# A chunked scan whose solve is made for two head pairs at once: one product with the states, one with block-diagonal inverses

## The chip, the cores and the metric

The kernel runs on one core of a Trainium2 chip. The metric is device microseconds of one execution; the time before is the median of three runs. A profile of one execution gives every instruction with its start and duration. The engines are named as in the profile: PE (TensorE, its matmuls), PEld (TensorE's weight loads), DVE (VectorE), ACT (ScalarE), POOL (GpSimd) and SP, whose queue issues the DMAs.

## The reference

One layer of a hybrid decoder over 528 positions (16 learned ones ahead of 512), width 2048, all fp32. The change touches the recurrence of its 16 heads of size 64, `rwkv7_scan`:

```python
# S_t = S_{t-1} diag(w_t) + (S_{t-1} a_t) b_t^T + v_t k_t^T ; y_t = S_t r_t
def step(s, inp):
    r_t, w_t, k_t, v_t, a_t, b_t = inp
    sa = jnp.einsum('bhvk,bhk->bhv', s, a_t)
    s = s * w_t[:, :, None, :] + sa[..., None] * b_t[:, :, None, :] + v_t[..., None] * k_t[:, :, None, :]
    y_t = jnp.einsum('bhvk,bhk->bhv', s, r_t)
    return s, y_t
```

Around it stand the layer's projections (`n @ w_in` with 6592 columns, `w_out`), a short convolution group beside the heads, a norm per head, and a feed-forward block (`w_gate_up`, a causal convolution, `w_down`).

## The kernel before, in words

Activations lie with features on partitions and time along the free axis. Every large product is made from splits of both operands (hi and lo, type float32r): three matmuls of 128x128 weights and about 258 moving columns for each tile, all into PSUM tiles named `mps`. The small products of the recurrence are plain fp32; such a matmul is two instructions in the trace.

**Pairs and chunks.** The 16 heads are 8 pairs P; a pair's two heads h lie on partitions 0 to 63 and 64 to 127. Two pairs (p = 0, 1) go through one scan s, so there are four scans, one after the other. Time is cut into NC = 17 chunks of C = 32 positions.

**prep(P)** fills `XR`, the moving side of the scan: for each head on its own 64 partitions the scaled vectors a (first 32 columns of a chunk) and r (last 32), and on the other 64 partitions their products with k and b, made by 64x64 matmuls (tile `aux`, from `bk`) and masked. **inverse(s)** turns the 68 small triangular matrices of a scan into their inverses on DVE and writes them to DRAM (`d2`); **inverses(s, i)**, called by `load`, brings them to the SBUF tile `AT` in two parts of 9 and 8 chunks, on SP's queue. **moves** copies k, b and v with transposes into `BK` and `VT`.

**scan(s)**, for every chunk c, works on `cur`, one of three tiles `SUV` of 128 x (2 pairs, 2 heads, 64): the state of a head on its own 64 partitions, and on the other 64 the values v (32 rows, put there by POOL) and the solved u (32 rows).

1. x0: for each pair one fp32 matmul with `cur[:, p]` as weights (128x128) and the chunk's a columns of both heads as 64 moving columns. The result lies with values on partitions; two DVE transposes of 64x64 bring the wanted blocks to `X0`.
2. u: for each pair one fp32 matmul of `AT` (128x128) with `X0`, 64 moving columns; four ACT copies of 32x64 bring u into `cur`.
3. State: four 64x64 matmuls (`BK` with `cur`), then DVE adds the decayed state `s0`, made by POOL, and writes the next `SUV`.
4. y: for each pair one fp32 matmul with `cur[:, p]` as weights and the r columns of both heads as 64 moving columns; two ACT copies write `yt`.

All four results are PSUM tiles named `st`, of which two are in turn.

**Order of the work.** Everything up to the output projection is only recorded first (`Plan.keep`). `Plan.order` then simulates the engines with the costs of `Plan.time` (an fp32 matmul of n columns in the full array counts n / 600 + 0.02 us, a matmul in a smaller mode 0.055, a change of mode 0.1 or 0.25) and gives out all instructions in the order found: work of the scan, prep, inverse and norm comes first when it is ready, and projection matmuls (`rkv`, `conv`, rank FILL) fill TensorE in between. After the last scan the norms of its two pairs (`head_norm`) run under the last projections, and the output projection follows. Nearly every instruction is recorded through one helper line, L218, so tiles are told apart by name.

Of the kernel before, what the change touches and what calls it, by code (L numbers as in the profile page):

```python
# [10 lines left out]
F32 = mybir.dt.float32  # L11
# [14 lines left out]
C = 32  # L26
# [195 lines left out]
class Plan:  # L222
# [51 lines left out]
    def time(self, x):  # L274

        e, op, out = x["engine"].name, x["op"], x["out"]
        n = 1
        for s in out.shape[1:] if isinstance(out, View) else (512,):
            n *= s
        psum = any(a.tile.pool.space == "psum" for a in x["ins"])  # L280
        if e == "PE":
            if self.mode(x) != (128, 128):
                return 0.055
            return n / 600 + 0.02 if x["args"][1].tile.dtype is F32 else n / 2400 + 0.0115
        if e == "SP":
            return 0.42
        if e == "POOL":
            if op == "memset":
                return 0.1 + 0.0008 * n
            if op == "tensor_scalar":  # L290
                return 0.3 + 0.0011 * n
            return 0.25 + 0.0019 * n if n > 300 else 0.2 + 0.0016 * n
        if e == "ACT":
            t = 0.15 + 0.00087 * n if psum else 0.19 + 0.00084 * n
            return t + (0.09 if isinstance(x["kw"].get("scale"), View) or isinstance(x["kw"].get("bias"), View) else 0)
        if op == "tensor_reduce":
            n = 1
            for s in x["kw"]["in_"].shape[1:]:
                n *= s
        if op == "tensor_tensor_scan":  # L300
            return 0.2 + 0.002 * n
        if op in ("tensor_scalar", "tensor_copy", "memset") and not psum:
            return 0.15 + 0.00055 * n
        if op == "transpose":
            return 0.19 + 0.00102 * n
        return 0.155 + 0.00104 * n + (0.06 if isinstance(x["kw"].get("scalar"), View) else 0)
# [167 lines left out]
def hymba(tc, I, out, ysp=None):  # L474
# [99 lines left out]
    with ExitStack() as ctx1:  # L574
# [8 lines left out]
            SUV.append(t)  # L583

        ATw = p1.tile([128, (2 * NC + 1) * 2 * C], F32, name="AT")
        G.memset(ATw, 0.0)
        AT = ATw[:, :NC * 4 * C].rearrange("r (c p b t) -> r c p b t", c=NC, p=2, b=2)
        X0 = []  # L590
        for i in range(2):
            t = p1.tile([128, 2, 2, C], F32, name=f"X0{i}")
            G.memset(t, 0.0)
            X0.append(t)

        xs = []
        ss = []
# [77 lines left out]
                PE.matmul(ps[:, :b - a], w, x[:, a:b], start=(i == 0), stop=(i == len(terms) - 1))  # L675
            return ps[:, :b - a]

        xr_shape = [128, 2, 2, NC, 64]
        lox = []

        def lora_in(t):
            if t == T_WD:
                wad = p1.tile(xr_shape, F32R, name="XR", bufs=2).rearrange("p a b c d -> p (a b c d)")
                wd, ad = inproj(t, HL), inproj(T_AD, HL, [
                    (wad[:, 1024 * i:1024 * i + 512], wad[:, 1024 * i + 512:1024 * i + 1024]) for i in range(KT // 4)])
                for _ in range(KT):
                    next(wd)
                    yield
                    if _ >= LAG:
                        next(ad)  # L690
                        yield
                for _ in range(max(0, LAG - LATE)):
                    next(ad)
                    yield
                ps0 = yield from wd
                rstd = p1.tile([128, L], F32, name="rstd")
                m, q = p1.tile([128, LP], F32, name="t1"), p1.tile([128, LP], F32, name="t2")
                for a, b in HL:
                    rms([x[:, a:b] for x in ss], rstd[:, a:b], m[:, a:b], q[:, a:b], aux, "aux")
                norm1.append(rstd)  # L700
                both = p1.tile(xr_shape, F32R, name="XR", bufs=2).rearrange("p a b c d -> p (a b c d)")
                lox.extend([both[:, i * L:i * L + L] for i in (2 * n, 2 * n + 1)] for n in range(4))
                tb = p1.tile([128, 2 * C * C + C], F32, name="tb")
                o = tb[:, :L]
                shift(ps0, t, o)
                S.activation(out=o, in_=o, func=AF.Tanh)
                split(o, *lox[0])
                o = tb[:, L:2 * L]
                shift((yield from ad), T_AD, o)
                split(o, *lox[1])  # L710
            else:
                o = p1.tile([128, 2 * C * C + C], F32, name="tb")[:, :L]
                yield from shifted(t, o)
                S.activation(out=o, in_=o, func=AF.Sigmoid)
                split(o, *lox[2 + t - T_GD])
# [42 lines left out]
        def prep(P):  # L758
            s, p = P // 2, P % 2
            if p == 0:  # L760
                st["s", s] = (p1.tile([128, 2, 2, NC, 64], F32, name="XR", bufs=2),
                              p1.tile([128, 2, NC], F32, name="PC", bufs=2))
            XR, PC = st["s", s]
            k, r, v = st.pop(("k", P)), st.pop(("r", P)), st.pop(("v", P))
# [36 lines left out]
            G.tensor_tensor(out=al, in0=kk, in1=al, op=ALU.mult)  # L801
            for h in range(2):
                q = slice(64 * h, 64 * h + 64)
                V.scalar_tensor_tensor(out=XR[q, h, p, :, :C], in0=chunked(kk[q]), scalar=-1.0,
                                       in1=Pp[q, :, :C], op0=ALU.mult, op1=ALU.mult)
            for h in range(2):
                q = slice(64 * h, 64 * h + 64)
                G.tensor_tensor(out=XR[q, h, p, :, C:], in0=chunked(r[q]), in1=Pp[q, :, 1:], op=ALU.mult)
            V.tensor_tensor(out=bk[:, :, :C], in0=chunked(k), in1=chunked(Pi), op=ALU.mult)
            V.tensor_tensor(out=bk[:, :, C:], in0=chunked(al), in1=chunked(Pi), op=ALU.mult)  # L810
            br = p1.tile([128, LP], F32, name="t3")
# [5 lines left out]
            for c0 in range(0, NC, 8):  # L817
                n = min(8, NC - c0)
                ps = aux.tile([128, 8, 64], F32, name="aux")
                for c in range(c0, c0 + n):  # L820
                    for h in range(2):
                        q = slice(64 * h, 64 * h + 64)
                        o = slice(64 - 64 * h, 128 - 64 * h)
                        PE.matmul(ps[o, c - c0], bk[q, c], XR[q, h, p, c], start=True, stop=True)
                for h in range(2):
                    o = slice(96 - 64 * h, 128 - 64 * h)
                    V.transpose(pt[32 - 32 * h:64 - 32 * h, c0:c0 + n], ps[o, :n, :C])
                    o = slice(64 - 64 * h, 128 - 64 * h)
                    V.tensor_tensor(out=XR[o, h, p, c0:c0 + n], in0=ps[o, :n],
                                    in1=gmask[o].unsqueeze(1).to_broadcast([64, n, 64]), op=ALU.mult)  # L830
                yield 0.05 * n * 2, PD3
            if p == 0:
                st["d1", s] = dp.tile([4 * NC, C, C], F32, name="d1", bufs=2)
# [3 lines left out]

            for h in range(2):
                q = slice(64 * h, 64 * h + 64)
                G.tensor_tensor(out=XR[q, h, p, 1:], in0=XR[q, h, p, 1:],  # L840
                                in1=PC[q, p, :NC - 1].unsqueeze(2).to_broadcast([64, NC - 1, 64]), op=ALU.mult)

            b_ = br[:, :L]
            for a, b, ps in blocksum(x):
# [36 lines left out]
        def inverses(s, i):  # L881
# [1 line left out]
            c0, c1 = CH[i]  # L883
            d2 = st["d2", s]
            for h in range(2):
                for b in range(2):
                    o = 64 * h + 32 * b
                    SP.dma_start(AT[o:o + 32, c0:c1, :, b].rearrange("s c p t -> s (c p) t"),
                                 d2[2 * (h * NC + c0):2 * (h * NC + c1)].rearrange("q s t -> s q t"))

        def piece(s, i, n):

# [68 lines left out]
        def scan(s):  # L961
# [4 lines left out]
            for c in range(NC):  # L966
# [8 lines left out]
                    if c == 0:  # L975
                        G.memset(cur[64 * h:64 * h + 64, :, h], 0.0)

                xp = stp.tile([128, 2, 2, C], F32, name="st")
                for p in range(2):
                    PE.matmul(xp[:, p], cur[:, p], XR[:, :, p, c, :C], start=True, stop=True)  # L980
                x0 = X0[c % 2]
                for h in range(2):
                    q = slice(64 * h, 64 * h + 64)
                    V.transpose(x0[q, :, h], xp[q, :, h])
                yield 0.2, D1 * f
                up = stp.tile([128, 2, 2, C], F32, name="st")
                for p in range(2):
                    w = 2 * C * (2 * c + p)
                    PE.matmul(up[:, p], ATw[:, w:w + 128], x0[:, p], start=True, stop=True)
                for h in range(2):  # L990
                    o = 96 - 64 * h
                    for b in range(2):
                        S.copy(cur[o:o + 32, :, h, C * b:C * b + C], up[C * b:C * b + C, :, h])
                yield 0.2, D2 * f
                if c == 1:
                    inverses(s, 1)
# [6 lines left out]
                if c < NC - 1:  # L1003
# [11 lines left out]
                    for h in range(2):  # L1015
# [2 lines left out]
                            V.tensor_tensor(out=nxt[q, :, h], in0=sp[q], in1=s0[q], op=ALU.add)  # L1018
                        else:
                            V.tensor_copy(nxt[q, :, h], sp[q])  # L1020
                yp = stp.tile([128, 2, 2, C], F32, name="st")
                for p in range(2):
                    PE.matmul(yp[:, p], cur[:, p], XR[:, :, p, c, C:], start=True, stop=True)
                n = min(C, L - c * C)
                for h in range(2):
                    q = slice(64 * h, 64 * h + 64)
                    S.copy(yt[q, :, c * C:c * C + n], yp[q, :, h, :n])
                if c == CH[0][1] - 1:
                    st["half", s] = True
                yield 0.75, D3 * f  # L1030
# [7 lines left out]
        def head_norm(P, tags):  # L1038
# [4 lines left out]
            ahead = P >= NP - 2  # L1043
            if ahead:
                if P % 2:
                    t = p1.tile(xr_shape, F32, name="XR", bufs=2).rearrange("p a b c d -> p (a b c d)")
                else:
                    t = p1.tile([128, 2 * C * C + C], F32, name="tb")
                bv, g = t[:, :L], t[:, L:2 * L]
# [819 lines left out]
```

## Time and profile before

| | |
|---|---|
| median of 3 runs | 2435.49 us (2435.47 to 2435.78) |
| profiled execution, its own time | 2438.57 us |
| its span in the profile | 2436.8 us |
| mean granted TensorE clock | 0.994 |
| PE busy | 2389.3 us (98%), 18546 matmul instructions |
| DVE busy | 1731.2 us (71%) |
| ACT busy | 1157.3 us (47%) |
| POOL busy | 659.0 us (27%) |
| the scans | from about 215 to 772 us of the span |

Rows of the timeline read: start in us, time from the first to the last instruction of the merged row, engine, line, operation, output tile <- input tiles, for matmuls the part of the array used (rows*columns), the shape, and the count. Rows of one tile read: count, then shortest/median/longest duration in ns, then first and last start in us. A row of waits reads: who waited for whom, us in total, times, longest. Because matmuls overlap, their cost is read from the starts of successive rows.

### The profile page before, as it was taken

How to read it: one execution, taken by the hardware profiler on the slowest of the kernel's cores; microseconds unless marked ns; L12 is line 12 of the kernel's file. 1: busy time of each engine (PE TensorE's matmuls, PEld its weight loads, DVE VectorE, ACT ScalarE, POOL GpSimd, SP SyncE). 2: the span in 40 equal slices, each digit the busy share in tenths (PEclk: the TensorE clock that was granted, in tenths of full speed). 3: DMA queues.
4: the chain of work that ended last, by engine and by line, in shares of the span. 5: the costliest groups of instructions: out<-in, count | busy, mean ns of one | idle time of the engine just before them, and what ended most of it. 6: DMA issues, size and time to landing. Idle time of an engine off the chain costs nothing.

```text
span 2436.8 us, 46251 instructions
## 1 busy us (share of the span) xinstructions
PE 2389.3 (98%) x18546; PEld 2283.9 (94%) x18546; DVE 1731.2 (71%) x2410; ACT 1157.3 (47%) x2139; POOL 659.0 (27%) x755
## 2 busy tenths in 40 slices
PE   7999999999999999999999999999999999999996
PEld 7999999999999999898999999998989898989896
DVE  6677888888865623786676767686868585959586
ACT  6666655656553433464443434343425252525254
POOL 2222646455442011441111212121212020202025
PEclk9999999999999999999999999999999999999998
DMA  5444332342442633423232324242424232323352
GB/s 175 148 130 123 89 88 82 101 110 86 119 124 77 201 92 120 153 84 104 78 122 85 122 75 127 70 130 70 138 70 130 78 122 87 110 90 103 98 193 71
DMA packets 138806, 266.64 MB, mean 109 GB/s; under 512 B 38592, under 2 KB 51648, under 8 KB 138592
## 3 DMA queue, kind: packets, MB, share of 16 engines
q1 hardware_dynamic: 138592, 263.69, 35.0%
q8 instruction: 146, 2.39, 0.4%
q14 instruction: 68, 0.56, 0.1%
HBM read 240.69 MB, written 22.95 MB: 108 GB/s over the span
## 4 chain that ended last, share of the span: by engine, by line
PE 90%; DVE 5%; DMA 2%; issue 1%; ACT 1%; SPq 0%; POOL 0%; DVEq 0%; ACTq 0%; POOLq 0%
PE mps L218 58%; PE u L218 16%; PE d L218 10%; PE st L218 5%; PE aux L218 2%; DVE acc L218 1%; DVE O L218 1%; DVE raw L218 1%; DMA raw<-w_in_dram 0%; DVE q L218 0%; DMA R<-w_down_dram 0%; DVE tt L218 0%; DMA l<-t 0%; DMA d<-tb 0%; PE psn L218 0%
## 5 line engine op out<-in xcount | busy, mean ns | idle before, releaser
L218 ACT CAST H<-R 128x1024 fp32r<-128x1024 f32 x373 | 391.9, 1051 | 455.3 <-PE u L218 172.6
L218 DVE TENSOR_TENSOR O<-R,H 128x1024 fp32r<-128x1024 f32 x373 | 488.9, 1311 | 109.8 <-ACT H L218 109.5
L218 PE MATMUL mps<-ahi,whi 128*128 128x258 f32 (+2 forms) x2048 | 406.1, 287 | 12.2 <-ACT whi L218 12.2
L218 PE MATMUL mps<-ahi,wlo 128*128 128x258 f32 (+2 forms) x2048 | 406.5, 287 | 1.7 <-DVE wlo L218 1.6
L218 PE MATMUL mps<-alo,whi 128*128 128x258 f32 (+2 forms) x2048 | 406.7, 287 | 0.3 <-DVE alo L218 0.3
L218 DVE TENSOR_TENSOR wlo<-raw,whi 128x512 fp32r<-128x512 f32 x289 | 209.2, 728 | 181.8 <-ACT whi L218 162.7
L218 PEld LDWEIGHTS mps<-ahi,whi 128*128 128x128 f32 x2048 | 311.1, 190 | 12.7 <-ACT whi L218 12.4
L218 PEld LDWEIGHTS mps<-ahi,wlo 128*128 128x128 f32 x2048 | 312.4, 190 | 2.4 <-DVE wlo L218 2.1
L218 PEld LDWEIGHTS mps<-alo,whi 128*128 128x128 f32 x2048 | 312.0, 190 | 0.9 <-DVE alo L218 0.5
L218 ACT CAST whi<-raw 128x512 fp32r<-128x512 f32 x289 | 178.2, 621 | 241.0 <-PE mps L218 187.5
L218 PE MATMUL mps<-tt,H 128*128 128x258 f32 x1968 | 263.3, 284 | 1.8 <-ACT q L218 1.8
L218 POOL TENSOR_TENSOR raw<-raw,rb 128x516 f32<-128x516 f32 (+1 forms) x45 | 92.8, 2064 | 627.5 <-DVE raw L218 583.5
L218 PE MATMUL mps<-alo,H 128*128 128x258 f32 x1032 | 255.2, 284 | 6.0 <-DVE alo L218 6.0
L218 PE MATMUL mps<-ahi,H 128*128 128x258 f32 x1032 | 255.1, 284 | 1.0 <-ACT q L218 1.0
L218 PEld LDWEIGHTS mps<-tt,H 128*128 128x128 f32 x1968 | 249.1, 190 | 2.0 <-ACT q L218 2.0
L218 POOL TENSOR_TENSOR R<-R 128x1024 f32<-128x1024 f32 x40 | 133.1, 3327 | 422.4 <-DVE R L218 422.4
L218 DVE TENSOR_TENSOR R<-R 128x1024 f32<-128x1024 f32 x120 | 209.0, 1741 | 1.1
L218 PEld LDWEIGHTS mps<-alo,H 128*128 128x128 f32 x1032 | 194.8, 190 | 6.8 <-DVE alo L218 6.2
L218 PEld LDWEIGHTS mps<-ahi,H 128*128 128x128 f32 x1032 | 195.4, 190 | 1.8 <-ACT q L218 1.2
L218 POOL TENSOR_SCALAR SUV<-VT 32x64 f32<-32x64 f32 x272 | 135.1, 497 | 206.7 <-PE st L218 181.1
L218 PE MATMUL mps<-ahi,O 128*128 128x258 f32 x1032 | 153.4, 284 | 0.0
L218 PE MATMUL mps<-tt,O 128*128 128x258 f32 x984 | 141.8, 283 | 0.0
(318 smaller groups left out, 4536.6 us busy)
## 6 DMA issues: line engine op xcount, KB each, us to landing
R<-w_gu_dram SPq DMA_DIRECT2D x176, 512.0 KB, 3.6
raw<-w_in_dram SPq DMA_DIRECT2D x208, 256.0 KB, 2.7
R<-w_down_dram SPq DMA_DIRECT2D x88, 512.0 KB, 4.4
raw<-w_out_dram SPq DMA_DIRECT2D x64, 256.0 KB, 2.6
l<-lo SPq DMA_DIRECT2D x24, 264.0 KB, 2.5
hsp<-acc SPq DMA_DIRECT2D x8, 512.0 KB
tt<-hsp SPq DMA_DIRECT2D x4, 1024.0 KB, 10.8
lo<-l SPq DMA_DIRECT2D x12, 264.0 KB, 3.5
```

What stands on the lines that cost most here:

```text
L218: return getattr(self.real, op)(*real, **{k: x.get() if isinstance(x, View) else x for k, x in kw.items()})
```

## The change

In the scan, x0 takes `XR`'s a columns of both pairs and both heads as weights (128 rows, 2 x 2 x 32 columns) and the whole of `cur` as 256 moving columns: one matmul. Of its result only the four diagonal blocks of 32x64 are used; four ACT copies put them one below another into `x0` (128 x 64), and the two transposes are gone. `AT` becomes one 128x128 block-diagonal matrix a chunk (four blocks of 32x32, one for each pair and head), and u is one matmul of it with `x0`. y is made by four matmuls, one for each pair and head, with `cur[:, p, h]` (128x64) as weights and 32 moving columns; the heads' results lie on partitions 0 to 63 and 64 to 127 (128x64 tiles of the array), and one ACT copy takes both. `XR` is laid out by chunk first; `AT` is loaded by as many DMAs, each of half the size, because no block is stored twice. The planner's cost of an fp32 matmul in the full array changes.

```diff
-            return n / 600 + 0.02 if x["args"][1].tile.dtype is F32 else n / 2400 + 0.0115
+            return max(0.222, n / 600 + 0.004) if x["args"][1].tile.dtype is F32 else n / 2400 + 0.0115
...
-        ATw = p1.tile([128, (2 * NC + 1) * 2 * C], F32, name="AT")
-        G.memset(ATw, 0.0)
-        AT = ATw[:, :NC * 4 * C].rearrange("r (c p b t) -> r c p b t", c=NC, p=2, b=2)
...
+        AT = p1.tile([128, NC, 2, 2, C], F32, name="AT")
+        G.memset(AT, 0.0)
...
-        xr_shape = [128, 2, 2, NC, 64]
+        xr_shape = [128, NC, 2, 2, 2, C]
...
-                V.scalar_tensor_tensor(out=XR[q, h, p, :, :C], in0=chunked(kk[q]), scalar=-1.0,
+                V.scalar_tensor_tensor(out=XR[q, :, 0, p, h], in0=chunked(kk[q]), scalar=-1.0,
...
-                G.tensor_tensor(out=XR[q, h, p, :, C:], in0=chunked(r[q]), in1=Pp[q, :, 1:], op=ALU.mult)
+                G.tensor_tensor(out=XR[q, :, 1, p, h], in0=chunked(r[q]), in1=Pp[q, :, 1:], op=ALU.mult)
...
             for h in range(2):
-                for b in range(2):
-                    o = 64 * h + 32 * b
-                    SP.dma_start(AT[o:o + 32, c0:c1, :, b].rearrange("s c p t -> s (c p) t"),
-                                 d2[2 * (h * NC + c0):2 * (h * NC + c1)].rearrange("q s t -> s q t"))
+                for p in range(2):
+                    o = 64 * p + 32 * h
+                    SP.dma_start(AT[o:o + 32, c0:c1, p, h],
+                                 d2[2 * (h * NC + c0) + p:2 * (h * NC + c1):2].rearrange("c s t -> s c t"))
...
-                xp = stp.tile([128, 2, 2, C], F32, name="st")
+                xp = stp.tile([128, 2, 2, 64], F32, name="st")
+                PE.matmul(xp, XR[:, c, 0].rearrange("r p h t -> r (p h t)"), cur, start=True, stop=True)
+                x0 = p1.tile([128, 64], F32, name="x0", bufs=2)
                 for p in range(2):
-                    PE.matmul(xp[:, p], cur[:, p], XR[:, :, p, c, :C], start=True, stop=True)
-                x0 = X0[c % 2]
-                for h in range(2):
-                    q = slice(64 * h, 64 * h + 64)
-                    V.transpose(x0[q, :, h], xp[q, :, h])
+                    for h in range(2):
+                        q = slice(64 * p + 32 * h, 64 * p + 32 * h + 32)
+                        S.copy(x0[q], xp[q, p, h])
                 yield 0.2, D1 * f
-                up = stp.tile([128, 2, 2, C], F32, name="st")
+                up = stp.tile([128, 64], F32, name="st")
+                PE.matmul(up, AT[:, c].rearrange("r p h t -> r (p h t)"), x0, start=True, stop=True)
                 for p in range(2):
-                    w = 2 * C * (2 * c + p)
-                    PE.matmul(up[:, p], ATw[:, w:w + 128], x0[:, p], start=True, stop=True)
-                for h in range(2):
-                    o = 96 - 64 * h
-                    for b in range(2):
-                        S.copy(cur[o:o + 32, :, h, C * b:C * b + C], up[C * b:C * b + C, :, h])
+                    for h in range(2):
+                        S.copy(cur[96 - 64 * h:128 - 64 * h, p, h], up[64 * p + 32 * h:64 * p + 32 * h + 32])
...
-                yp = stp.tile([128, 2, 2, C], F32, name="st")
+                yp = stp.tile([128, 2, C], F32, name="st")
                 for p in range(2):
-                    PE.matmul(yp[:, p], cur[:, p], XR[:, :, p, c, C:], start=True, stop=True)
+                    for h in range(2):
+                        q = slice(64 * h, 64 * h + 64)
+                        PE.matmul(yp[q, p], cur[:, p, h], XR[:, c, 1, p, h], start=True, stop=True)
                 n = min(C, L - c * C)
-                for h in range(2):
-                    q = slice(64 * h, 64 * h + 64)
-                    S.copy(yt[q, :, c * C:c * C + n], yp[q, :, h, :n])
+                S.copy(yt[:, :, c * C:c * C + n], yp[:, :, :n])
```

The other lines of the diff rewrite reads and writes of `XR` for its new layout.

More of the change, by code (lines that the diff above doesn't have):

```diff
@@ L583, in hymba @@
             SUV.append(t)
-        ATw = p1.tile([128, (2 * NC + 1) * 2 * C], F32, name="AT")
-        G.memset(ATw, 0.0)
-        AT = ATw[:, :NC * 4 * C].rearrange("r (c p b t) -> r c p b t", c=NC, p=2, b=2)
[L590 to L594, printed above, removed]
+        AT = p1.tile([128, NC, 2, 2, C], F32, name="AT")
+        G.memset(AT, 0.0)
         xs = []
@@ L682, in lora_in @@
             if t == T_WD:
-                wad = p1.tile(xr_shape, F32R, name="XR", bufs=2).rearrange("p a b c d -> p (a b c d)")
+                wad = p1.tile(xr_shape, F32R, name="XR", bufs=2).rearrange("r c a p h t -> r (c a p h t)")
                 wd, ad = inproj(t, HL), inproj(T_AD, HL, [
@@ L700, in lora_in @@
                 norm1.append(rstd)
-                both = p1.tile(xr_shape, F32R, name="XR", bufs=2).rearrange("p a b c d -> p (a b c d)")
+                both = p1.tile(xr_shape, F32R, name="XR", bufs=2).rearrange("r c a p h t -> r (c a p h t)")
                 lox.extend([both[:, i * L:i * L + L] for i in (2 * n, 2 * n + 1)] for n in range(4))
@@ L760, in prep @@
             if p == 0:
-                st["s", s] = (p1.tile([128, 2, 2, NC, 64], F32, name="XR", bufs=2),
+                st["s", s] = (p1.tile(xr_shape, F32, name="XR", bufs=2),
                               p1.tile([128, 2, NC], F32, name="PC", bufs=2))
@@ L823, in prep @@
                         o = slice(64 - 64 * h, 128 - 64 * h)
-                        PE.matmul(ps[o, c - c0], bk[q, c], XR[q, h, p, c], start=True, stop=True)
+                        PE.matmul(ps[o, c - c0], bk[q, c], XR[q, c, :, p, h], start=True, stop=True)
                 for h in range(2):
@@ L828, in prep @@
                     o = slice(64 - 64 * h, 128 - 64 * h)
-                    V.tensor_tensor(out=XR[o, h, p, c0:c0 + n], in0=ps[o, :n],
-                                    in1=gmask[o].unsqueeze(1).to_broadcast([64, n, 64]), op=ALU.mult)
+                    V.tensor_tensor(out=XR[o, c0:c0 + n, :, p, h], in0=ps[o, :n].rearrange("q c (a t) -> q c a t", a=2),
+                                    in1=gmask[o].rearrange("q (a t) -> q a t", a=2).unsqueeze(1).to_broadcast(
+                                        [64, n, 2, C]), op=ALU.mult)
                 yield 0.05 * n * 2, PD3
@@ L839, in prep @@
                 q = slice(64 * h, 64 * h + 64)
-                G.tensor_tensor(out=XR[q, h, p, 1:], in0=XR[q, h, p, 1:],
-                                in1=PC[q, p, :NC - 1].unsqueeze(2).to_broadcast([64, NC - 1, 64]), op=ALU.mult)
+                xd = XR[q, 1:, :, p, h]
+                G.tensor_tensor(out=xd, in0=xd, in1=PC[q, p, :NC - 1].unsqueeze(2).unsqueeze(3).to_broadcast(
+                    [64, NC - 1, 2, C]), op=ALU.mult)
             b_ = br[:, :L]
@@ L1045, in head_norm @@
                 if P % 2:
-                    t = p1.tile(xr_shape, F32, name="XR", bufs=2).rearrange("p a b c d -> p (a b c d)")
+                    t = p1.tile(xr_shape, F32, name="XR", bufs=2).rearrange("r c a p h t -> r (c a p h t)")
                 else:
```

## The prediction, made before the change was run

> **What bounds the kernel now.** I read the page first (span, chain of waits), then the windows over the scan, then what TensorE waited for there, then the instructions on the PSUM tile `st`, which only the scan uses, then TensorE's timeline.
>
> ```profile
> span 2436.8 us, 46251 instructions
> PE 90%; DVE 5%; DMA 2%; issue 1%; ACT 1%; SPq 0%; POOL 0%; DVEq 0%; ACTq 0%; POOLq 0%
> ```
>
> ```profile
> sum 557.00, PE 554.76 PEld 538.27 DVE 431.45 ACT 318.09 POOL 276.99; mean PE 138.69 PEld 134.57 DVE 107.86 ACT 79.52 POOL 69.25
> ```
>
> ```profile
> PE st L218 <- DMA AT<-d: 1.8, 1, 1.8
> PE st L218 <- DVE X L218: 0.3, 1, 0.3
> ```
>
> The chain that ended last is TensorE for 90%. The second view is the sum over the four scans, 215 to 772 us: TensorE has work in 554.8 of 557 us. The third is every wait of TensorE from 215 to 840 us: 2.1 us. The four scans (68 chunks, 8.2 us each on average) run inside projection matmuls that fill the gaps, so a chunk's cost is the time it takes away from that stream, not its latency. The chunk's instructions, all 68 together:
>
> ```profile
> L218 PE MATMUL st<-XR,SUV x544: 217/275/324, 152.1 to 771.8; 128*128 128x64 f32 x182
> L218 PE MATMUL st<-SUV,BK x512: 218/218/267, 221.5 to 766.1; 64*64 64x64 f32 x171
> L218 PE MATMUL st<-X,AT x272: 217/275/324, 216.7 to 769.7; 128*128 128x64 f32 x136
> L218 ACT COPY SUV<-st x272: 200/203/208, 218.6 to 770.6; 32x64 f32<-32x64 f32 x136
> L218 DVE STREAM_TRANSPOSE X<-st x136: 200/248/256, 166.5 to 768.6; 64x64 f32<-64x64 f32 x136
> L218 ACT COPY yt<-st x136: 180/208/212, 222.6 to 772.3; 64x64 f32<-64x64 f32 x128, 64x32 f32<-64x32 f32 x8
> ```
>
> One fp32 matmul is two instructions: 544 for the x0 and y products together is 4 matmuls a chunk. Durations (275 ns) overlap, so costs are taken from starts.
>
> **The change, part by part.** *Price of the old groups.* A pair of projection matmuls takes 0.24 us from start to start (first two rows below):
>
> ```profile
> 564.68 0.41 PE L218 MATMUL mps<-ahi,wlo 128*128 128x258 f32 x2
> 564.92 0.40 PE L218 MATMUL mps<-ahi,whi 128*128 128x258 f32 x2
> 565.17 0.55 PE L218 MATMUL st<-XR,SUV 128*128 128x64 f32 x4
> 565.53 0.49 PE L218 MATMUL mps<-alo,whi 128*128 128x258 f32 x2
> 565.85 0.41 PE L218 MATMUL mps<-ahi,wlo 128*128 128x258 f32 x2
> ```
>
> From 564.92 to 565.85 is 0.93; less two projection pairs (0.48) the x0 group costs 0.45 us, two matmuls of 0.22 with 64 moving columns. The u group has the same form and count.
>
> *x0: two matmuls become one with 256 moving columns.* The nearest row is the norm's sum, four fp32 matmuls of 264 columns:
>
> ```profile
> 32.69 0.61 PE L218 MATMUL psn<-sg,ones 128*128 128x264 f32 x2
> ...
> 34.71 0.40 PE L218 MATMUL mps<-alo,XR 128*128 128x264 f32 x2
> ```
>
> From the first of the eight to the second projection pair after them, 32.69 to 34.71, is 2.02, less a projection pair 1.78, so 0.445 each, and 0.43 at 256 columns. The x0 group thus goes from 0.445 to 0.43: -0.01 us a chunk. Four times the columns cost no more because a 64-column matmul costs 0.22 here whatever it streams.
>
> *u: two matmuls become one of the same form:* -0.22 us a chunk.
>
> x0 and u together: -0.23 x 68 = -15.6 us.
>
> *y: two full matmuls become four of 128 rows by 64 columns with 32 moving columns.* They follow the four 64x64 state matmuls:
>
> ```profile
> 765.57 0.40 PE L218 MATMUL mps<-ahi,wlo 128*128 128x258 f32 x2
> 765.90 0.46 PE L218 MATMUL st<-SUV,BK 64*64 64x64 f32 x8
> 766.28 0.66 PE L218 MATMUL st<-XR,SUV 128*128 128x64 f32 x4
> 766.75 0.72 PE L218 MATMUL mps<-ahi,whi 128*128 128x258 f32 x4
> 767.31 0.28 PE L218 MATMUL mps<-alo,whi 128*128 128x258 f32 x1
> ```
>
> 765.57 to 767.31 is 1.74, less a pair and four single projection matmuls (0.24 + 0.48): state and y cost 1.02 now. What of this is the change of array mode comes from two groups of 64x64 matmuls in the preparation, of 4 and of 64 instructions:
>
> ```profile
> 153.55 0.40 PE L218 MATMUL mps<-ahi,whi 128*128 128x264 f32 x2
> 153.88 0.33 PE L218 MATMUL aux<-XR,bk 64*64 64x64 f32 x4
> 154.14 0.52 PE L218 MATMUL mps<-alo,whi 128*128 128x264 f32 x2
> 154.50 0.41 PE L218 MATMUL mps<-ahi,wlo 128*128 128x264 f32 x2
> ```
>
> ```profile
> 148.21 0.41 PE L218 MATMUL mps<-alo,whi 128*128 128x264 f32 x2
> 148.55 2.08 PE L218 MATMUL aux<-XR,bk 64*64 64x64 f32 x64
> 150.56 0.51 PE L218 MATMUL mps<-ahi,wlo 128*128 128x264 f32 x2
> 150.91 0.41 PE L218 MATMUL mps<-ahi,whi 128*128 128x264 f32 x2
> ```
>
> The small group costs 0.95 - 0.48 = 0.47, the large one 2.70 - 0.48 = 2.22. The difference, 1.75 over 30 matmuls, is 0.058 a matmul; what is left of the small one, 0.47 - 2 x 0.058 = 0.35, is entering and leaving the mode, 0.175 a change. Check: 4 x 0.058 + 0.35 + 0.445 = 1.03, against 1.02.
>
> No row shows 128x64. Its matmul is bounded by 0.058 (like 64x64) and 0.22 (like the full array, 64 columns). The 64x64 matmul is 3.8 times cheaper than the full one; half the weight columns can give 2, and the two heads on two tiles at once the other 2. y has half the columns too, and its two heads write different halves of the columns. I take 0.058. A change from 64x64 to 128x64 is also unseen: between 0 and 0.35 (a whole round trip), I take 0.175, as each other change. Then state and y cost 0.233 + 0.233 + 3 x 0.175 = 0.99, -0.03 in each of the 64 chunks that have both; the last chunk of a scan has y alone, 0.233 + 0.35 - 0.445 = +0.14, four times. Together -1.4 us.
>
> The Trainium skill speaks for this and against it. *TensorEngine Tiling (Array Packing)*, section Key Properties, says that tiles load weights and multiply in parallel and that changing the mode drains the array, which the 0.35 agrees with. *TensorE: Matmul & The Clock Gate*, section The mechanism (what overlaps and what doesn't), says that a weight load runs under a matmul in flight only when the row groups differ. The two tiles of y share all rows, so by that rule they would take turns, which is the first rival; by the first page the sum stays as above.
>
> *Copies.* Two DVE transposes (2 x 0.248) become four ACT copies of 32x64 (4 x 0.203, the row of the copies to SUV, same shape), and two y copies (0.208 each) become one over 128 partitions. DVE: -0.50 a chunk, 34 us off 431. ACT: +0.60 a chunk, 41 us on 318 of 557 (57% to 64%). Neither is on the path as long as TensorE waits for nothing; the chunk's latency grows by 0.81 - 0.50 = 0.31, less 0.23 of TensorE's own. Queued behind the copies on ACT are the casts of the next weights; they are late only if the plan puts them late. Without that cover the 0.08 costs 5 us over 68 chunks. The scan's cover at its end:
>
> ```profile
> 772.12 0.37 ACT L218 COPY yt<-st 64x32 f32<-64x32 f32 x2 [1.28 <-PE st L218]
> 796.89 0.67 ACT L218 ACTIVATE Pi<-aux 128x264 f32<-128x264 f32 x2 [2.23 <-PE aux L218]
> 825.19 0.64 ACT L218 ACTIVATE lo<-Pi 128x528 f32<-128x528 f32 x1
> 831.90 0.62 ACT L218 CAST ahi<-k 128x514 fp32r<-128x514 f32 x1 [2.97 <-DVE k L218]
> ```
>
> The last scan ends at 772.5 and the last pair's norm lies idle from 797.6 to 825.2. That is 27.6 us of slack; TensorE coming 17 us earlier uses part of it and leaves 10.
>
> *Rest, taken as nothing.* The inverses go to AT in as many transfers of half the size; the one wait for them (1.8 us) can shrink, nothing to -1.8. SP's queue keeps its number of issues. XR's writes on DVE and POOL keep their elements and runs of 32; if the new strides slowed them, DVE's lost 34 us would cover it, and behind those stands the same slack. The zeroing of X0 falls away ahead of the first matmul. The planner counts an fp32 matmul of 64 columns at 0.127 before and 0.222 after, so the whole order is drawn anew.
>
> Sum: -15.6 - 1.4 = -17 us. The profiled execution's span is 2436.8 and its own time 2438.57, 3.1 above the median of the runs, 2435.49. I take the difference from the median: **2418 us**. The unseen mode change at 0 or at 0.35 moves this by 64 x 0.175 = 11 each way: 2407 to 2430.
>
> **The rivals.** *The y tiles take turns (serial).* One stream then costs twice 0.058, y 0.467: +0.233 x 68 = +15.9, and the net is -1: 2434. For it: both tiles need the same 128 rows for weights and data. Against: nothing in the trace. If what sets the 0.22 is the 128 rows and not the columns, y costs 4 x 0.22 = 0.89, +0.655 x 68 = +44.5, net +28: 2463. By the skill's *TensorE: Matmul & The Clock Gate*, section LDWEIGHTS, it is columns (its 107 ns for 128 agrees with 0.111 an instruction here), and eight loads of 64 in turn would be an estimated 0.43.
>
> *The scan becomes the bound (slower).* If each x0 copy waits behind one more ACT instruction, such as a weight cast, a chunk is longer by 0.31 + 0.62 - 0.23 = 0.70:
>
> ```profile
> L218 ACT CAST whi<-raw 128x512 fp32r<-128x512 f32 x137 | 84.1, 621 | 83.9 <-PE mps L218 69.1 <-issue 9.0 <-DMA raw<-w_in_dram 1.8
> ```
>
> 68 x 0.70 = 48, less the slack of 27.6: the last norm would come 20 us later than TensorE needs it now, 2455. It decides from (27.6 + 4.9) / 68 = 0.48 a chunk. For it: the shortest chunks have little spare, the last one takes 5.71 between its u groups:
>
> ```profile
> 763.70 0.55 PE L218 MATMUL st<-X,AT 128*128 128x64 f32 x4
> 769.41 0.55 PE L218 MATMUL st<-X,AT 128*128 128x64 f32 x4
> ```
>
> Against: the mean chunk is 8.2, so most of it is waiting behind other work, on DVE above all, and DVE gets 34 us lighter.
>
> *The new order brings new stalls on TensorE.* The old plan thought TensorE quicker than it is, by 2 x (0.445 - 0.253) a chunk for x0 and u, 26 us in all; every other engine was early against it. The new plan takes that cushion away. Half of the gain lost, 0.13 a chunk: 2427.
>
> **How the numbers follow.** Parallel tiles 0.53 (2407 to 2430, at 2418), serial 0.20 (2431 to 2438), row-bound 0.05, scan-bound 0.12 (2430 to 2455), new stalls 0.10 (2420 to 2440). 0.2% of 2435.5 is 4.9 us, about what a measurement of this kernel tells from no change. Faster: 0.53, a fifth of serial, six tenths of the stalls, a tenth of scan-bound: 0.64. Slower: row-bound, three quarters of scan-bound, two tenths of the stalls: 0.16. The range 2406 to 2437 holds the first, most of the second, most of the stalls and some of the scan-bound case, 0.8.
>
> **What would show it.** Right: one x0 group of 2 instructions costing 0.43, u 0.22, state and y 0.99 from the same kind of starts; no transposes on `st`; TensorE's waits between 215 and 840 still near 2 us; the last `st` matmul some 15 us earlier or at least no later. Wrong: y instructions 0.05 or more apart throughout (serial) or 0.11 apart (row-bound); TensorE waiting for ACT on `st` tiles (stalls), or for the last pair's split after the scan (scan-bound).

## The result, and the profile after

| | before | after |
|---|---|---|
| median | 2435.48 us (2435.07 to 2435.78, 4 runs) | 2418.92 us (2417.87 to 2420.04, 4 runs) |
| ratio, 95% interval | | 0.9932 [0.9915, 0.9949] |
| profiled execution: own time, span | 2438.57, 2436.8 us | 2420.04, 2417.9 us |

16.6 us faster, against a forecast of 17. The page after:

```profile
span 2417.9 us, 46262 instructions
PE 2365.9 (98%) x18546; PEld 2253.1 (93%) x18546; DVE 1700.5 (70%) x2274; ACT 1195.3 (49%) x2343; POOL 670.8 (28%) x753
PE 90%; DVE 5%; DMA 2%; issue 1%; ACT 1%; POOL 0%; SPq 0%; DVEq 0%; ACTq 0%; POOLq 0%
```

TensorE is still 90% of the chain, with the same 18546 matmul instructions as before: two fewer for x0 and two fewer for u in each chunk, four more for y. What a chunk issues has changed as written. The instructions on the tile `st`, all 68 chunks:

```profile
L218 PE MATMUL st<-XR,SUV x544: 222/223/243, 219.7 to 739.5; 128*64 128x32 f32 x182
L218 ACT COPY x<-st x272: 185/204/209, 149.9 to 736.5; 32x64 f32<-32x64 f32 x136
L218 PE MATMUL st<-SUV,XR x136: 377/378/483, 149.3 to 735.4; 128*128 128x256 f32 x136
L218 PE MATMUL st<-x,AT x136: 217/273/324, 214.6 to 737.3; 128*128 128x64 f32 x136
L218 ACT COPY yt<-st x68: 186/213/215, 221.2 to 739.8; 128x64 f32<-128x64 f32 x64, 128x32 f32<-128x32 f32 x4
```

The count is on the right of the name (544 small y instructions, 136 for x0, 136 for u), the copies take 204 and 213 ns, near the 203 and 208 that were reckoned with, and the transposes are gone. Over the whole span DVE's busy time falls by 30.7 us and ACT's rises by 38.0, near the 34 and 41 forecast. The last y matmul starts at 739.5 where it started at 771.8: the scans end 32 us earlier, so the scan is no nearer to being the bound.

The price of each group, from starts in TensorE's timeline of the changed kernel (a chunk of the last scan, two stretches):

```profile
721.25 0.40 PE L218 MATMUL mps<-alo,whi 128*128 128x258 f32 x2
721.58 0.46 PE L218 MATMUL st<-SUV,BK 64*64 64x64 f32 x8
721.97 0.42 PE L218 MATMUL st<-XR,SUV 128*64 128x32 f32 x8
722.32 0.51 PE L218 MATMUL mps<-ahi,wlo 128*128 128x258 f32 x2
722.67 0.40 PE L218 MATMUL mps<-ahi,whi 128*128 128x258 f32 x2
...
723.38 0.40 PE L218 MATMUL mps<-ahi,wlo 128*128 128x258 f32 x2
723.62 0.59 PE L218 MATMUL st<-SUV,XR 128*128 128x256 f32 x2
723.86 0.59 PE L218 MATMUL mps<-alo,whi 128*128 128x258 f32 x2
724.29 0.40 PE L218 MATMUL mps<-ahi,whi 128*128 128x258 f32 x2
```

```profile
725.49 0.41 PE L218 MATMUL mps<-alo,whi 128*128 128x258 f32 x2
725.73 0.33 PE L218 MATMUL st<-x,AT 128*128 128x64 f32 x2
725.87 0.48 PE L218 MATMUL mps<-ahi,whi 128*128 128x258 f32 x2
726.19 0.40 PE L218 MATMUL mps<-alo,whi 128*128 128x258 f32 x2
```

Each stretch less two projection pairs (0.48): state and y 1.42 - 0.48 = 0.94, x0 0.91 - 0.48 = 0.43, u 0.70 - 0.48 = 0.22. Before they cost 1.02, 0.445 and 0.445. One chunk stands for the others: read the same way wherever such a group lies free between two projection pairs, the medians of the trace are 0.939 (51 groups), 0.435 (55) and 0.227 (54), and in the kernel before 1.030, 0.449 and 0.449.

A row merges several instructions. Those of y in the first stretch start at 721.967, 721.974, 722.046, 722.053, 722.104, 722.111, 722.163 and 722.169: in pairs 7 ns apart, with 58 to 79 ns from pair to pair. They are not 0.05 us apart throughout, as two tiles that take turns would be.

And TensorE's waits, from 130 to 840 us:

```profile
PE st L218 <- DMA AT<-d: 4.9, 3, 2.1
PE st L218 <- DVE SUV L218: 2.9, 3, 1.2
PE st L218 <- ACT SUV L218: 0.5, 1, 0.5
PE st L218 <- ACT VT L218: 0.4, 1, 0.4
PE st L218 <- ACT x L218: 0.3, 1, 0.3
```

That is 9.0 us, where the kernel before had 2.1. (7.7 of it lies after 215 us, the figure in one expectation below; the longest stand at the starts of scans, where TensorE is ready for the first u before the inverses have landed.) Most of it is for these transfers and for DVE; ACT, which the prediction named as the sign of stalls, has 1.2 us of it. Totals of waits here and below can differ by 0.1 from the sum of their rows, which are rounded.

### The profile page after: what moved, and what is told of

It is laid out like the page before. It is cut to its first block, busy times and chain, and to the rows that moved or that the text cites. A ratio compares the mean times of both kernels' runs of the same rounds, so it can differ in the third digit from the quotient of the medians.

```text
span 2417.9 us, 46262 instructions
## 1 busy us (share of the span) xinstructions
PE 2365.9 (98%) x18546; PEld 2253.1 (93%) x18546; DVE 1700.5 (70%) x2274; ACT 1195.3 (49%) x2343; POOL 670.8 (28%) x753
## 4 chain that ended last, share of the span: by engine, by line
PE 90%; DVE 5%; DMA 2%; issue 1%; ACT 1%; POOL 0%; SPq 0%; DVEq 0%; ACTq 0%; POOLq 0%
PE mps L218 58%; PE u L218 16%; PE d L218 10%; PE st L218 4%; PE aux L218 2%; DVE acc L218 1%; DMA raw<-w_in_dram 1%; DVE raw L218 1%; DVE q L218 0%; DVE O L218 0%; DVE alo L218 0%; DVE tt L218 0%; DVE wlo L218 0%; DMA d<-tb 0%; DMA AT<-d 0%
## 5 line engine op out<-in xcount | busy, mean ns | idle before, releaser
L218 PE MATMUL mps<-ahi,whi 128*128 128x264 f32 (+2 forms) x2048 | 411.2, 289 | 10.2 <-ACT whi L218 10.0
L218 PE MATMUL mps<-alo,whi 128*128 128x264 f32 (+2 forms) x2048 | 407.7, 287 | 0.2 <-DVE alo L218 0.2
L218 POOL TENSOR_SCALAR SUV<-VT 32x64 f32<-32x64 f32 x272 | 144.3, 531 | 137.0 <-PE st L218 109.7
```

Source lines behind the costliest of these rows:

```text
L218: return getattr(self.real, op)(*real, **{k: x.get() if isinstance(x, View) else x for k, x in kw.items()})
```

## The experiments

The runs stand in three groups of four. "Under before" is against the kernel before in the same group, 2433.23, 2433.91 and 2433.34 us in the median.

**e1, the kernel before with the new planner cost**

```diff
-            return n / 600 + 0.02 if x["args"][1].tile.dtype is F32 else n / 2400 + 0.0115
+            return max(0.222, n / 600 + 0.004) if x["args"][1].tile.dtype is F32 else n / 2400 + 0.0115
```

> The kernel before with one line changed: the planner counts an fp32 matmul in the full array as the changed kernel does (at least 0.222 us). The instructions are the same, their order is drawn anew. Theory (TensorE's issue time is the bound): no instruction is cheaper, so within 5 us of before, 2432 to 2440, and TensorE's waits on the scan's tiles may rise by a few us because the plan loses its cushion. Rival (the new plan makes the gain): about 2420.

Measured: 2441.49 us, ratio 1.0029 [1.0017, 1.0040], 8.3 us slower. The new plan makes no gain; it makes waits, as the theory had it, but the loss is more than the 5 us expected, and the time 1.5 us over the range given. TensorE's waits, 130 to 800 us:

```profile
PE st L218 <- DMA AT<-d: 3.7, 3, 1.7
PE aux L218 <- DVE t L218: 1.7, 2, 0.9
PE st L218 <- DVE X L218: 1.1, 2, 0.5
PE st L218 <- DVE SUV L218: 0.8, 2, 0.5
PE mps L218 <- DVE wlo L218: 0.6, 1, 0.6
PE st L218 <- ACT SUV L218: 0.4, 1, 0.4
```

8.3 us in place of 2.1, with the instructions unchanged.

**e2, the changed kernel with the old planner cost** (the same line turned back)

> The changed kernel with the planner's old cost (n / 600 + 0.02). Theory: the instructions keep their gain of some 22 us; with the old cushion back the new waits on the scan's tiles (7.7 us in the changed kernel, 2.1 before) fall, so 2413 to 2419. Rival (the new plan makes the gain): back to about 2435. If the waits stay, the cushion is not what they come from.

Measured: 2412.81 us, ratio 0.9914 [0.9901, 0.9928], 20.4 under before, just under the range given. The waits, 130 to 800 us:

```profile
PE st L218 <- DMA AT<-d: 0.8, 1, 0.8
PE st L218 <- ACT x L218: 0.8, 2, 0.4
PE st L218 <- ACT zm L218: 0.6, 1, 0.6
PE st L218 <- ACT whi L218: 0.2, 1, 0.2
```

2.4 us are left of 9.0. The gain is in the instructions, and the plan that came with them takes some of it back: 3.8 us, though the intervals of the two ratios still overlap.

**e3, y as before**

```diff
-                yp = stp.tile([128, 2, C], F32, name="st")
+                yp = stp.tile([128, 2, 2, C], F32, name="st")
                 for p in range(2):
-                    for h in range(2):
-                        q = slice(64 * h, 64 * h + 64)
-                        PE.matmul(yp[q, p], cur[:, p, h], XR[:, c, 1, p, h], start=True, stop=True)
+                    PE.matmul(yp[:, p], cur[:, p], XR[:, c, 1, p], start=True, stop=True)
```

(and two copies of 64 partitions in place of one).

> The changed kernel with y as before: two full matmuls of 64 columns and two copies. Theory: state and y go back from 0.93 to 1.02 us a chunk, 68 times 0.09: 6 us slower than the changed kernel, about 2425. Rival (y is worth nothing, as the prediction's sum nearly had it): 1 us slower, 2420.

Measured: 2418.85 us, ratio 0.9939 [0.9926, 0.9951], 14.4 under before. By time the expectation failed: each against the kernel before in its own group, e3 is 2.2 us behind the changed kernel, not 6, and the two intervals overlap. Its starts show the higher price of y:

```profile
692.10 0.41 PE L218 MATMUL mps<-alo,whi 128*128 128x258 f32 x2
692.44 0.46 PE L218 MATMUL st<-SUV,BK 64*64 64x64 f32 x8
692.82 0.66 PE L218 MATMUL st<-XR,SUV 128*128 128x64 f32 x4
693.29 0.49 PE L218 MATMUL mps<-alo,whi 128*128 128x258 f32 x2
693.62 0.64 PE L218 MATMUL mps<-ahi,wlo 128*128 128x258 f32 x4
```

1.52 - 0.48 = 1.04 a chunk, as before. But this order of the work has only 4.3 us of waits: 5 us lost at y, 4.7 us fewer waits.

**e4, y of both heads on one tile of the array**

```diff
-                yp = stp.tile([128, 2, C], F32, name="st")
+                yp = stp.tile([64, 2, 2, C], F32, name="st")
...
-                        PE.matmul(yp[q, p], cur[:, p, h], XR[:, c, 1, p, h], start=True, stop=True)
+                        PE.matmul(yp[:, p, h], cur[:, p, h], XR[:, c, 1, p, h], start=True, stop=True)
```

(and two copies from partitions 0 to 63).

> The changed kernel with the y of both heads on one and the same 128x64 tile of the array (both results on partitions 0 to 63, two copies spread them). Theory (the two tiles run at once in the changed kernel): the four matmuls now take turns, y's stream goes from 0.23 to 0.47 us, 68 times 0.23 is 16: about 2435. Rival (they took turns already): no change, 2419, and the starts within y stay as they were.

Measured: 2426.18 us, ratio 0.9969 [0.9958, 0.9981], 7.1 under before, 9.5 less gained than in the changed kernel. In the timeline:

```profile
692.01 0.40 PE L218 MATMUL mps<-alo,whi 128*128 128x258 f32 x2
692.34 0.45 PE L218 MATMUL st<-SUV,BK 64*64 64x64 f32 x8
692.72 0.65 PE L218 MATMUL st<-XR,SUV 128*64 128x32 f32 x8
693.30 0.51 PE L218 MATMUL mps<-ahi,wlo 128*128 128x258 f32 x2
693.65 0.41 PE L218 MATMUL mps<-ahi,whi 128*128 128x258 f32 x2
```

1.64 - 0.48 = 1.16 against 0.94: +0.22 a chunk, 15 us, the price of taking turns to 0.01. From y's first start to the next group it is 0.58 here and 0.35 in the changed kernel. The single instructions of y start one by one here, 79 and then 58 or 59 ns apart, where they came in pairs. So in the changed kernel the two tiles do run at once. The time is 9 us under the 2435 expected; the waits, 3.5 us here, are 5.5 fewer and account for the greater part of that.

**e5, u by two matmuls of 32 columns, old planner cost**

```diff
-                PE.matmul(up, AT[:, c].rearrange("r p h t -> r (p h t)"), x0, start=True, stop=True)
+                for i in range(2):
+                    PE.matmul(up[:, C * i:C * i + C], AT[:, c].rearrange("r p h t -> r (p h t)"), x0[:, C * i:C * i + C],
+                              start=True, stop=True)
```

> The changed kernel with the planner's old cost, and with u made again by two matmuls, each of 32 moving columns. Theory (an fp32 matmul in the full array costs 0.22 us for any number of columns up to about 130): the u group costs 0.445 again, 68 times 0.22 is 15 us more than the changed kernel with the old cost (21 us under before), so 6 us under before. Rival (the cost follows the columns, 64 in all as before): no more than 2 us slower, 19 to 21 under before.

Measured: 2429.72 us, ratio 0.9983 [0.9974, 0.9992], 4.2 under before and 16 behind e2. The same 64 columns in two matmuls cost the full price twice:

```profile
694.76 0.40 PE L218 MATMUL mps<-ahi,whi 128*128 128x258 f32 x2
695.01 0.53 PE L218 MATMUL st<-x,AT 128*128 128x32 f32 x4
695.37 0.49 PE L218 MATMUL mps<-alo,whi 128*128 128x258 f32 x2
695.70 0.40 PE L218 MATMUL mps<-ahi,wlo 128*128 128x258 f32 x2
```

0.94 - 0.48 = 0.46, with half the columns each: at 32 and 64 columns the price goes by the matmul. The 130 columns in the theory are an estimate, the 0.445 us of a matmul with 264 columns taken down in proportion to 0.22; no run here tests a number of columns in between.

**e6, x0's copies on DVE, old planner cost** (`V.tensor_copy` in place of `S.copy`)

> The changed kernel with the planner's old cost, and with the four copies of x0 on DVE in place of ACT: DVE gets some 0.9 us a chunk back (before, two transposes took 0.50) and ACT loses 0.82. Theory (TensorE's issue time alone counts): within 4 us of the changed kernel with the old cost, 17 to 25 us under before. Rival (the lighter DVE makes part of the gain): 8 us or more lost of the 21.

Measured: 2417.61 us, ratio 0.9936 [0.9924, 0.9949], 16.3 under before. 4 us are lost against e2, just outside the theory's range and half of what the rival asked. TensorE's waits are 6.4 us, 4 more than e2's, with the x0 copies, now on DVE, the largest (2.4 us). So DVE's load, 57 us more than e2's over the span (1755.4 us against 1698.4), costs 4 us here, about what the waits grew by.

**e7, the inverses' transfers planned to land 2.5 us later**

```diff
-        return self.pipe + LAND + (2.0 if a.parts == 4 * NC else 0)
+        return self.pipe + LAND + (2.0 if a.parts == 4 * NC else 2.5 if a is x["out"] and a.parts == 32 else 0)
```

> The changed kernel with one planner figure more: it takes the inverses' transfers into AT to land 2.5 us later than it did. Theory (the new plan is too tight): TensorE's waits for these transfers (4.9 us in the changed kernel) fall under 1, some 4 us faster than it: 20 to 21 us under before. Rival (the waits come from the transfers themselves, whatever the plan): they stay.

Measured: 2423.54 us, ratio 0.9956 [0.9944, 0.9969], 10.4 under before: a miss. The waits for AT are gone, as expected, but others took their place, 9.2 us in all, of which 2.0 us for ACT's x0 copies are the largest. Mending one wait draws the whole order anew, and here the new order was no better.

**e8, the planner's margin before a matmul 0.6 us in place of 0.3** (`GAP`), new cost

> The changed kernel with the planner's margin before a matmul that follows another engine raised from 0.3 to 0.6 us; the new cost stays. Theory (the lost cushion makes the new waits): TensorE's waits between 130 and 840 us fall from 8.9 to 4 or less, 3 to 6 us faster than the changed kernel, 19 to 22 under before. Rival (the new cost of itself gives a worse order): no faster than the changed kernel, 15 to 17 under before.

Measured: 2415.18 us, ratio 0.9924 [0.9911, 0.9938], 18.7 under before. The waits fall to 4.4 us, just over the figure given, and those for AT are gone; the time, 2.1 us better than the changed kernel's, is just short of the theory's range and outside the rival's.

**e9, e10, e12: controls, the order drawn anew** (`HOP`, the delay from one engine to another that the planner assumes, for TensorE 0.7 in place of 0.6; it enters the priorities alone), and **e11, both cushions** (old cost, `GAP` 0.6)

> A control: the changed kernel (new cost) with the order drawn anew by a figure that enters the priorities alone, not the planned times (HOP of TensorE 0.6 to 0.7). Theory (the new cost takes a cushion from the plan): TensorE's waits between 130 and 800 us stay at 6 to 10, 13 to 18 us under before. Rival (each drawing of the order is a throw of the dice, whatever the cost): waits anywhere from 2 to 10.

> The same control with the planner's old cost. Theory: waits stay at 2 to 4, 18 to 23 us under before. Rival (a throw of the dice): waits of 5 or more are as likely as here.

> The changed kernel with the planner's old cost and the margin of 0.6: both cushions. Theory: waits 2 or less, 20 to 24 us under before, no more than 2 us better than the old cost alone, since that left 2.3 us of waits. Rival: the larger margin holds the scan back so that it ends later than the projections can hide, and time is lost.

> The same control on the kernel before (old cost). Theory: waits 2 to 4 and within 4 us of before. Rival (a throw of the dice): up to 8 us slower, as with the new cost.

Measured: e9 2414.45 us, 0.9926 [0.9913, 0.9938], waits 6.3; e10 2415.15 us, 0.9923 [0.9910, 0.9935], waits 3.4; e11 2413.58 us, 0.9918 [0.9904, 0.9931], waits 3.3; e12 2432.83 us, 0.9998 [0.9989, 1.0007], waits 1.8.

With the instructions of the changed kernel the waits are 9.0 and 6.3 us under the new cost, 2.4 and 3.4 under the old one; with those of the kernel before, 8.3 under the new cost, 2.1 and 1.8 under the old one. That is the cushion's side. The variants do not keep to it: under the new cost e3 and e4 have 4.3 and 3.5 us, under the old one e5 has 3.7 and e6 6.4. And on the changed kernel the old cost is a small cushion: by its formula it counts u 0.127 us where 0.222 is taken, but x0 0.447 where 0.43 is taken, 0.08 us a chunk or 5 us in all, against the 26 us of the kernel before. So the cushion is the likelier reading, and that each drawing of the order is a throw of the dice is not excluded.

e9's gain lay just above the range given; e11's waits were 3.3 and not 2, its gain just under its range, and the larger margin brought nothing on top of the old cost. In time, the one order drawn with the new cost on the kernel before is slower clear of noise (e1 1.0029 [1.0017, 1.0040], e12 0.9998), but on the changed kernel the cushion is not separable from a redrawing of the order: e9 with the new cost is as fast as e10 with the old.

**All runs in one table.** Issue is the change in TensorE's price (x0 -1.0, u -15.1, y -4.7), waits are those from 130 to 800 us less the 2.1 of before.

| | issue | waits | sum | measured, us against before |
|---|---|---|---|---|
| changed kernel | -21 | +6.9 | -14 | -16.6 |
| e1 | 0 | +6.2 | +6 | +8.3 |
| e2 | -21 | +0.3 | -21 | -20.4 |
| e3 | -16 | +2.2 | -14 | -14.4 |
| e4 | -21 + 15 | +1.4 | -5 | -7.1 |
| e5 | -21 + 15 | +1.6 | -4 | -4.2 |
| e6 | -21 | +4.3 | -17 | -16.3 |
| e7 | -21 | +7.1 | -14 | -10.4 |
| e8 | -21 | +2.3 | -19 | -18.7 |
| e9 | -21 | +4.2 | -17 | -18.9 |
| e10 | -21 | +1.3 | -20 | -18.2 |
| e11 | -21 | +1.2 | -20 | -19.8 |
| e12 | 0 | -0.3 | 0 | -0.5 |

Two numbers per kernel give the time of thirteen kernels within 4 us, most within 3. So the term of the instructions, up to 21 us, is well tested, and that of the waits, 7 us at most, only roughly. Waits outside the stretch are not in the table: over the whole span they add up to 28.5 us before and 33.6 after, +5.1 and not +6.9. What is left is not settled; the clock (below) may be a part.

## Why the prediction was right, point by point

The total came out 0.9 us from the forecast, and part of that is luck: two terms were off by 3 and 7 us, in opposite directions, and the nearly 3 us between the table's sum of -14 and the measured -16.6 made up the rest.

- *TensorE is the bound, a chunk costs what it takes from the stream.* Borne out by the table; the opposite view, that DVE's lighter load makes the gain, is refuted by e6 for all but 4 us.
- *x0 -0.01, u -0.22.* Measured 0.43 and 0.22, as forecast to 0.01; e5 shows that the 0.22 goes by the matmul, with 32 columns as with 64, and one with 256 columns replaces two with 64 for nothing.
- *State and y 0.99, -1.4 us in all.* Mis-sized: 0.94. The stream price 0.058 held, and e4 shows that it needs both tiles at once. Too high was the price of the change between two small modes: 0.94 - 2 x 0.233 - 0.35 is 0.12, not 0.175. (The single starts agree: from the last state instruction, 721.819, to y's first it is 0.148, of which a step of the stream is 0.029.) y brings 64 x 0.08, less 4 x 0.10 for the last chunks, where y stands alone (in the last scan from the projections' start at 738.71 over y's at 739.28 to 740.22, 1.51 less eight single projection matmuls of 0.12, is 0.55 against the old 0.445). Together -4.7 us, or -5.4 by the medians, in place of -1.4.
- *The serial rival* is refuted by e4 and by the starts in pairs, for these tiles. The Trainium skill's *TensorE: Matmul & The Clock Gate*, section The mechanism, says that a weight load runs under a matmul in flight only when the row groups differ. Taken as the prediction took it, that would have the changed kernel's y cost what e4's does, 0.58 to the next group and not 0.35; the measurement decides against it for two column tiles. (The same section of the Trainium skill also lets a load go ahead into a background weight buffer.) The Trainium skill's *TensorEngine Tiling (Array Packing)*, section Key Properties, fits both measurements: it says that tiles work in parallel, as y's do here, and that a change of mode drains, which goes with the 0.12 and the 0.35.
- *The row-bound price, 0.22 a y matmul,* is refuted: even in turns it is about 0.113 (e4: 0.22 over four, on top of 0.058).
- *The scan becomes the bound.* Refuted: the scans end 32 us earlier, and the last pair's norm lies idle from 776.3 to 807.1, 30.8 us where it was 27.6. The prediction's reckoning of this slack was wrong all the same: it had TensorE's gain use 17 us of it up and leave 10, and it had the last `st` matmul come some 15 us earlier. Why the new order ends the scans as early as it does stays open. The norm's last cast, at 831.90 before, came 18 us earlier with the rest:

```profile
813.71 0.62 ACT L218 CAST ahi<-k 128x514 fp32r<-128x514 f32 x1 [2.97 <-DVE k L218]
```

- *TensorE's waits near 2 us.* Wrong: 9.0. The rival of the new stalls happened beside the forecast, at 6.9 of the 8.5 us that it was given; its ground, the cushion that the too low cost left in the plan, is supported by e1 against e12 and by the waits of e2, e9 and e10, but not shown (e3, e4 and e6 above). That AT's smaller transfers could only shorten a wait was wrong too: its waits went from 1.8 to 4.9; with the old cost they are 0.8 (e2) and 2.5 (e10), and on the kernel before the new cost alone makes them 3.7 (e1).

So by the prices the change was worth 21 us, and 20 of them are had with the planner's old cost line (e2, the fastest median of all: 0.9914 [0.9901, 0.9928]).

## What to carry to other kernels

Where one engine is never idle, price a change by starts of successive instructions, per group and with the change of mode around it; durations overlap (275 ns for an instruction that costs 111 here), so adding them up would not have given these prices. In this kernel an fp32 matmul with 32 columns costs as much as one with 64, 0.22 us, and one with 256 no more than two of those, so merging narrow matmuls into a wide one was free even where most of the result is thrown away. And a planner's cost that is too low may be the margin that keeps the engine from waiting: correct it together with the margin, and look at the waits after every redrawing.

## What the runs showed of the hardware that was not expected

A single wait of 2.1 us was followed by a loss beyond itself. After the wait for AT at 498 us of the changed kernel, TensorE's pairs go from 0.24 us from start to start to 0.37 and then 0.44:

```profile
498.05 0.41 PE L218 MATMUL st<-x,AT 128*128 128x64 f32 x2 [2.13 <-DMA AT<-d]
...
499.33 0.41 PE L218 MATMUL mps<-alo,whi 128*128 128x264 f32 x2
499.57 0.57 PE L218 MATMUL mps<-ahi,whi 128*128 128x264 f32 x2
499.94 0.64 PE L218 MATMUL mps<-ahi,wlo 128*128 128x264 f32 x2
500.38 0.64 PE L218 MATMUL mps<-alo,whi 128*128 128x264 f32 x2
```

The eight pairs from 499.57 to 503.02 take 3.45 us where eight of 0.24 take 1.9, so about 1.5 us are lost there on top of the wait's 2.1. The granted clock of the stretch is 0.50 (the figure behind the busy times):

```profile
499.70:503.00 3.30, 3.30 (x17) 3.30 (x16) 1.29 (x1) 2.11 (x6) 2.32 (x2) 0.50 0.30 82
```

The kernel before had the same after its wait of 1.8 us that ended at 216.7, and e7 after one of 1.9. In e1 such a stretch at 597 us followed waits of 0.6 and 0.4 us, while waits of 1.9 us (e9) and 1.7 us (e6) passed without one. So the length of the wait alone does not decide, and what sets off such a stretch stays open.
